# When q and k are transposed, and where four modulation vectors are made, in a two-layer transformer on one core

## The chip, the cores and the metric

The kernel runs on one core of one Trainium2 chip. The metric is the device time of one execution in microseconds (us), and the number to predict is its median over several runs.

## The reference, cut to what matters

Two layers work on 256 latent and 256 context tokens of width 1024. Six modulation vectors per layer come from a small matrix product with a 1024 x 6144 weight. Layer 0 is attention beside a convolution and a dense feed-forward stage; layer 1 is a state-space mixer (S5) and a mixture of experts.

```python
def adaln(cond, w, b):
    return jnp.split(jax.nn.silu(cond) @ w + b, 6, axis=-1)
...
def na_conv_mixer(h_lat, h_ctx, w_in, q_g, k_g, ...):
    def project(h):
        q, k, v, a, g = jnp.split(h @ w_in, [512, 1024, 1536, 2048], axis=-1)
        return rmsnorm(heads(q), q_g), rmsnorm(heads(k), k_g), heads(v), a, g
    ...
    y_lat = concat(neighbourhood_attention(ql, kl, vl, kc, vc, rpb), conv_module(al, gl, ...)) @ w_out
    y_ctx = concat(context_attention(qc, kc, vc), conv_module(ac, gc, ...)) @ w_out
...
for l in range(2):
    sh1, sc1, g1, sh2, sc2, g2 = adaln(c, ada_w[l], ada_b[l])
    ...
    x_lat = x_lat + g1 * y_lat
    x_lat = x_lat + g2 * ffn(modulate(rmsnorm(x_lat, norm2_g[l]), sh2, sc2))
```

## The kernel before

All matrix products of the big weights are done as three products of split operands (`mm3`, lines 223 to 225): a weight tile of 1 MB is cast on ScalarE (`wh`, line 203), and the rest of it (`wl`, line 205) is formed on VectorE or GpSimd. In the profile and here PE, DVE, ACT, POOL and SP are TensorE, VectorE, ScalarE, GpSimd and SyncE.

**Weights.** `Stream` hands out four buffers of 1 MB (`raw`). `plan` lists the loads in order; SP issues each as soon as a buffer is free, in that order. A buffer comes free when its weight has been split, or, for a modulation weight (`ada`), when PE has used it.

**Modulation vectors.** A vector (l, v) has two halves n, and a half two loads j of 1 MB: a *unit* (l, v, n, j). `ada_unit` does four matmuls of 32 x 512 on one unit, side by side in four column groups, into one PSUM bank `ada`; after j = 1 `ada_out` copies the bank to `adsb` on ACT (line 373), and `ada_to_dram` (line 435) writes the half to a scratch tensor by a DMA that ACT issues. The jobs wait in one list (`fill`), and `ada_step` takes the next if its load has been issued. The vectors (1, 2) to (1, 5) are needed after the feed-forward stage.

**The first projection** (`mix_in`): for n in 3, 4, 0, 1, 2 (a, g, q, k, v) and two halves kh of the depth, four steps k of 12 matmuls of 512 columns, into four banks `mi`; PSUM has eight banks. After g, `glu` transposes `aT` (`uT`, line 592) and the taps of the convolution begin (`conv`): 93 on DVE (lines 674 and 676, `cv`), 31 by ACT and POOL (`ptap`, line 685). After q and after k, ACT squares the four banks (line 655), DVE sums them (`qss`, line 656), forms a reciprocal root from small operations and multiplies the banks by it (`qn`, line 658); the banks stay taken until then. `turn_qk` then transposes `qn` on PE (`qT`, line 601) and ACT copies it (line 602). It is called in the middle of the next projection:

```python
if rest and k == 1 and (kh if n else not kh):
    rest()
```

**Order.** ACT, POOL and SP follow the program's text here (`ORDERED`, "mix"); PE and DVE are ordered by a scheduler when the kernel is built. Every engine then runs its queue strictly in that order. In attention (`scores`, `raised`, ...), twelve jobs each need maxima on DVE (line 760 or 765), and the rest of the taps and the units of layer 0 lie between.

**The feed-forward stage** (`ffn`): eleven steps u, each with w1 and w3, and w2 four times. Between them lie the tables of S5: `pool_job` on POOL (`bst`, line 1179), `dve_job` on DVE, `pe_job` on PE (`g1T`, line 1210, and `kk`, line 1219). Units are done after w1 of steps below `ADAU` and in the stage's tail (`tail`, `TAIL`).

Of the kernel before, what the change touches and what calls it, by code (L numbers as in the profile page):

```python
# [33 lines left out]
def unit(w, k0, nk):  # L34

    return w[:, k0:k0 + nk]
# [120 lines left out]
class Kernel:  # L157
# [80 lines left out]
    def plan(self):  # L238
        a, st = self.a, self.st
        self.g1d = self.dram.tile([P, 64 * 256], F32, name="g1d")  # L240
        self.g2d = self.dram.tile([P, 64 * 256], F32, name="g2d")
        self.rowsd = self.dram.tile([4, D], F32, name="rowsd")
        self.partd = self.dram.tile([4, 4 * D], F32, name="partd")
        self.gated = [[self.dram.tile(shape, F32, name="gated") for shape in ([4, 2 * D], [2, D])] for _ in range(2)]
        self.kd = self.dram.tile([16, 64 * 240], F32, name="kd")
        mi = lambda n, kh: st.add(("mi", n, kh), unit(a["mix_w_in"][n], 4 * kh, 4))
        mix = lambda n: [mi(n, kh) for kh in range(2)]
        part = lambda l, v, n, j: st.add(("ada", l, v, n, j), unit(a["ada_w"][l, 2 * v + n], 4 * j, 4))
        ada = lambda l, v: [part(l, v, n, j) for n in range(2) for j in range(2)]
        for n in range(2):  # L250
            for v in range(2):
                for j in range(2):
                    part(0, v, n, j)
            mi(3, n)
        mix(4), mix(0), mix(1), mix(2)
        for qt in range(2):
            st.add(("bias", qt), a["bias"][:, qt])
        ada(0, 2), ada(0, 3), ada(0, 4)
        for kh in (1, 0):
            for n in range(2):  # L260
                st.add(("mo", n, kh), unit(a["mix_w_out"][n], 4 * kh, 4))
        halves = [(l, v, n) for l, v in ((0, 5), (1, 0), (1, 1), (1, 2), (1, 3), (1, 4), (1, 5)) for n in range(2)]

        def half():
            l, v, n = halves.pop(0)
            for j in range(2):
                part(l, v, n, j)
        for u in range(11):
            st.add(("w1", u), a["ffn_w1"][u])
            if u < 9:  # L270
                half()
            st.add(("w3", u), a["ffn_w3"][u])
            if u < 3:
                half()
            if u in FFN_ENDS:
                lo, hi = FFN_ENDS[u]
                for n in range(2):
                    for f in range(lo, hi, 4):
                        st.add(("w2", f, n), unit(a["ffn_w2"][n], f, min(4, hi - f)))
        half(), half()  # L280
        for j in range(2):
            for kh in range(2):
                st.add(("si", j, kh), a["ssm_w_in"][j, kh].rearrange("p r k f -> p r (k f)"))
        for b in range(8):
            st.add(("g1", b), self.g1d[:, b * UNIT:(b + 1) * UNIT])
        k = self.kd
        add_k = lambda b: st.add(("k", b), bass.AP(tensor=k.tensor, offset=k.offset + b * 16 * 240,
                                                   ap=[[16, 8], [64 * 240, 16], [240, 16], [1, 128]]))
        add_g2 = lambda b: st.add(("g2", b), self.g2d[:, b * UNIT:(b + 1) * UNIT])
        def add_so(j, dh, *zs):  # L290
            for z in zs:
                st.add(("so", dh, j, z), a["ssm_w_out"][dh, j, z])
        add_so(0, 0, 0, 1)
        for b in range(2):
            add_k(b)
        for b in range(4):
            add_g2(b)
        for b in (2, 3):
            add_k(b)
        add_g2(4), add_g2(5)  # L300
        add_so(0, 1, 0)
        add_g2(6), add_g2(7)
        add_so(0, 1, 1)
        for dh in range(2):
            add_so(1, dh, 0, 1)
        self.moe_plan()
# [270 lines left out]
    def mix_in(self, second):  # L577
# [19 lines left out]
        def turn_qk(n, qn):  # L597
            for pr in range(4):
                pt = self.ps("qT")
                for t in range(4):  # L600
                    nc.tensor.transpose(pt[:, t * P:(t + 1) * P], qn[:, t, pr * P:(pr + 1) * P], self.ident)
                nc.scalar.activation(self.qk[:, n, pr], pt, AF.Copy, scale=gains[n])

        rest, first = None, []
        for i, (n, kh) in enumerate(order):
            for j in (i, i + 1) if i else ():
                if j < len(order):
                    self.split(("mi",) + order[j])
            if kh == 0:
                pb = [self.ps("mi") for _ in range(4)]  # L610
            for k in range(4):
                bh, bl = self.piece(("mi", n, kh), k, 0, 512)
                kk = kh * 4 + k
                for t in range(4):
                    s = slice(t * P, (t + 1) * P)
                    self.mm3(pb[t], self.hh[:, kk, s], self.hl[:, kk, s], bh, bl, kk == 0, kk == 7)
                    if not i:
                        for _ in range(START.count((k, t))):
                            second.pop(0)()
                        if (k, t) == SPLIT1:  # L620
                            self.split(("mi", 3, 1))
                if first:
                    first.pop(0)()
                if rest and k == 1 and (kh if n else not kh):
                    rest()
                    rest = None
                if i:
                    self.pump(t=10, v=MIXV[n] if n < 3 else 0, p=MIXP[n] if n < 3 else 0)
            if not i:
                self.load_params(nc.scalar)  # L630
            if not i:
                self.qk = mp.tile([P, 2, 4, 512], F32, name="qk", tag="qk")
                self.v = mp.tile([P, 4, 512], F32, name="v", tag="v")
            self.drop(("mi", n, kh))
            if kh == 0:
                continue
            if n == 3:
                for t in range(4):
                    nc.scalar.copy(aT[:, t], pb[t])
            elif n == 4:  # L640
                for t in range(4):
                    g = self.wk([P, 512], "gt", 2)
                    nc.scalar.activation(g, pb[t], AF.Tanh, scale=0.5)
                    nc.vector.scalar_tensor_tensor(aT[:, t], g, 1.0, aT[:, t], op0=OP.add, op1=OP.mult)
                rest = glu
            elif n == 2:
                for t in range(4):
                    nc.scalar.copy(self.v[:, t], pb[t])
            else:
                qn = mp.tile([P, 4, 512], F32, name="qn", tag="big")  # L650
                ss = self.wk([P, 32], "qss", 1)
                heads = lambda y: y.rearrange("p (h d) -> p h d", h=8)
                for t in range(4):
                    sq = self.wk([P, 512], "gt", 2)
                    nc.scalar.activation(sq, pb[t], AF.Square)
                    nc.vector.tensor_reduce(ss[:, t * 8:t * 8 + 8], heads(sq), axis=AX.X, op=OP.add)
                rs = self.rsqrt(ss, 32, 64)
                first = [lambda t=t, y=pb[t], q=qn, r=rs[:, t * 8:t * 8 + 8]: nc.vector.tensor_tensor(
                    heads(q[:, t]), heads(y), r[:, :, None].to_broadcast([P, 8, 64]), op=OP.mult) for t in range(4)]
                rest = lambda n=n, qn=qn: turn_qk(n, qn)  # L660
# [66 lines left out]
    def attention(self):  # L727
# [76 lines left out]
        n = len(jobs)  # L804
        soft, pTs, out = {}, {}, None
        fill = [(m, t) for m in range(2) for t in range(4)]
        for i in range(n + 3):
# [2 lines left out]
            if i - 2 in soft:  # L810
                pTs[i - 2] = turn_p(soft.pop(i - 2))
            ss = scores(*jobs[i]) if i < n else None
            if i and len(self.vec) < 6:
                self.ada_step()
            self.pump(v=TAPS[0], p=TAPS[1])
            if ss:
# [108 lines left out]
    def ffn(self, g2b, norm):  # L925
# [20 lines left out]
        for u in range(11):  # L946
            lo = max([0] + [hi for e, (_, hi) in FFN_ENDS.items() if e < u])
            for which in ("w1", "w3"):
# [8 lines left out]
                else:  # L957
# [5 lines left out]
                    banks.clear()  # L963
                if which == "w1" and u < ADAU or u < 3:
                    self.ada_step()
# [1219 lines left out]
    def layer0(self):  # L2185
# [3 lines left out]
        sh2 = self.const.tile([P, 2, 8, 2], F32, name="shsc2")  # L2189
        shs = self.const.tile([P, 2, 8, 2], F32, name="shsc3")  # L2190
        gates = lambda: self.gates
        self.ada_to_rows(0, 2, gates)
        for i, v in enumerate((3, 4)):
            self.ada_to_cols(0, v, sh2[:, i], C_AB + 16 + 8 * i)
        self.ada_to_rows(0, 5, gates)
        for i in range(2):
            self.ada_to_cols(1, i, shs[:, i], C_AB + 32 + 8 * i)
        for i, v in enumerate((2, 3, 4, 5)):
            self.ada_to_dram(1, v, i)
        with tc.tile_pool(name="l0", bufs=1) as self.l0:  # L2200
            self.s5_params(self.l0.tile([P, 32, 64], F32, name="room", tag="gates"))
            self.hh, self.hl = self.halves()
# [79 lines left out]
MIXP = (1, 1, 3)  # L2282
ADDS = ((0,), (1,), (2,), (3,), (4,), (5,))
TAIL = (0, 0, 2, 0, 1, 1)
ADAU = 10
EARLY = (4, ('si', 0, 0))
START = ((1, 3), (1, 3), (1, 3), (3, 1))
SPLIT1 = (2, 3)
# [34 lines left out]
```

## Time and profile before

| | us |
|---|---|
| median of 3 runs | 1869.29 (1868.2 to 1874.53) |
| the profiled execution's own time | 1870.19 |
| its span in the profile | 1868.4 |

The profile is of one execution. Engine times are busy times; a wait is put down to the instruction that ended it. The projection lies between about 45 and 185 us of the span, attention between 185 and 260, the feed-forward stage between 330 and 785, S5 and the experts behind it.

### The profile page before, as it was taken

To read this page: it belongs to the slowest core of one execution; us is meant where nothing else is said; L and a number is where in the kernel's file an instruction comes from. 1 tells how busy PE (TensorE), PEld (TensorE's weight loads), DVE (VectorE), ACT (ScalarE), POOL (GpSimd) and SP (SyncE) were. 2 spreads that over 40 slices of the span, in tenths; PEclk is the share of its full clock that TensorE was granted. 3 is DMA by queue.
4 is the path that set the end of the run, shared out by engine and by line. 5 is a ranking of instruction groups with operands and counts; after the bars stand their busy time and mean duration, and the time that the engine had idled before them with its cause. 6 is when DMAs were issued, how large, how long until landed. Compare 5 with 4: busy or idle time off the path is not lost.

```text
span 1868.4 us, 23796 instructions
## 1 busy us (share of the span) xinstructions
PE 1725.3 (92%) x8730; PEld 1188.6 (64%) x8730; DVE 1249.1 (67%) x1709; ACT 803.0 (43%) x1156; POOL 474.6 (25%) x528
## 2 busy tenths in 40 slices
PE   6977898998989999897589999999999999999997
PEld 4855376876767778675478666556565656565653
DVE  4999797576675754769788565656565656565653
ACT  3434664332332332547456445344543435443540
POOL 2347057395893900245241000000000000000000
PEclk9988999999999999998799999999999999999999
DMA  7320734753645543449868899999999999998996
GB/s 319 131 73 23 278 123 152 255 193 125 220 157 177 194 160 113 160 159 176 251 272 330 340 419 419 404 386 387 420 420 381 385 390 420 417 387 356 407 420 273
DMA packets 107437, 517.08 MB, mean 277 GB/s; under 512 B 13792, under 2 KB 41696, under 8 KB 48688
## 3 DMA queue, kind: packets, MB, share of 16 engines
q1 hardware_dynamic: 76672, 490.77, 68.5%
q10 hardware_dynamic: 29968, 22.57, 3.8%
q0 software_dynamic: 672, 2.14, 0.4%
q8 instruction: 71, 1.16, 0.2%
q14 instruction: 54, 0.44, 0.1%
HBM read 496.46 MB, written 18.97 MB: 276 GB/s over the span
## 4 chain that ended last, share of the span: by engine, by line
PE 56%; DVE 7%; POOL 2%; DMA 2%; issue 1%; ACT 1%; ACTq 0%; SPq 0%; DVEq 0%; POOLq 0%
PE m L2022 11%; PE m L223 5%; PE y L2056 5%; PE m L224 5%; PE m L225 5%; PE y L224 3%; PE y L223 3%; PE y L225 3%; PE w L224 3%; PE w L223 3%; PE w L225 3%; DVE wl L205 1%; PE xT L1850 1%; PE gT L2041 1%; PE sc L1940 1%
## 5 line engine op out<-in xcount | busy, mean ns | idle before, releaser
L203 ACT CAST wh<-raw 128x1024 fp32r<-128x1024 f32 x192 | 194.6, 1049 | 155.1 <-PE w L225 74.7
L205 DVE TENSOR_TENSOR wl<-raw,wh 128x1024 fp32r<-128x1024 f32 x171 | 215.9, 1298 | 37.2 <-ACT wh L203 37.0
L2022 PE MATMUL m<-raw,E 128*64 128x512 f32 x392 | 177.9, 596 | 0.0
L2044 ACT CAST small<-gT 128x512 fp32r<-128x512 f32 x28 | 16.4, 586 | 300.3 <-PE gT L2041 300.3
L224 PE MATMUL w<-hl,wh 128*128 128x512 f32 (+1 forms) x384 | 144.1, 375 | 1.2 <-POOL hl L568 0.6
L223 PE MATMUL w<-hh,wh 128*128 128x512 f32 (+1 forms) x384 | 145.2, 379 | 0.0
L225 PE MATMUL w<-hh,wl 128*128 128x512 f32 (+1 forms) x384 | 142.8, 373 | 0.0
L224 PE MATMUL m<-wl,small 128*128 128x512 f32 x336 | 131.1, 390 | 1.0 <-DVE wl L205 1.0
L223 PE MATMUL m<-wh,small 128*128 128x512 f32 x336 | 131.4, 391 | 0.0
L225 PE MATMUL m<-wh,small 128*128 128x512 f32 x336 | 130.8, 389 | 0.0
L2045 DVE TENSOR_TENSOR small<-gT,small 128x512 fp32r<-128x512 f32 x28 | 19.4, 692 | 156.8 <-ACT small L2044 156.8
L2022 PE MATMUL m<-xres,E 128*64 128x512 f32 x216 | 98.5, 598 | 0.0
L2022 PEld LDWEIGHTS m<-raw,E 128*64 128x64 f32 x392 | 51.0, 137 | 66.5 <-issue 66.4
L1844 POOL TENSOR_SCALAR brow<-pw,order 128x128 fp32r<-128x128 f32 x6 | 5.5, 930 | 310.2 <-PE bk L1879 310.2
L223 PEld LDWEIGHTS w<-hh,wh 128*128 128x128 f32 x384 | 72.7, 189 | 17.3 <-issue 4.0
L224 PEld LDWEIGHTS w<-hl,wh 128*128 128x128 f32 x384 | 72.8, 189 | 15.0 <-POOL hl L568 2.8
L224 PE MATMUL w<-wl,gh 128*128 128x512 f32 x176 | 72.1, 410 | 10.4 <-DVE wl L205 10.4
L225 PEld LDWEIGHTS w<-hh,wl 128*128 128x128 f32 x384 | 72.5, 189 | 12.9
L205 POOL TENSOR_TENSOR wl<-raw,wh 128x1024 fp32r<-128x1024 f32 x21 | 53.2, 2543 | 100.3 <-ACT wh L203 100.3
L205 DVE TENSOR_TENSOR wl<-U,wh 128x1024 fp32r<-128x1024 f32 x55 | 67.3, 1262 | 13.2 <-ACT wh L203 13.1
L223 PE MATMUL w<-wh,gh 128*128 128x512 f32 x176 | 71.8, 408 | 2.0 <-ACT wh L203 2.0
L223 PEld LDWEIGHTS m<-wh,small 128*128 128x128 f32 x336 | 63.1, 188 | 15.2 <-ACT more L203 2.3
(440 smaller groups left out, 4474.1 us busy)
## 6 DMA issues: line engine op xcount, KB each, us to landing
raw<-in_moe SPq DMA_DIRECT2D x134, 1024.0 KB, 10.1
U<-in_moe SPq DMA_DIRECT2D x70, 1024.0 KB, 9.8
room<-in_moe SPq DMA_DIRECT2D x68, 1024.0 KB, 8.4
raw<-in_ada_w SPq DMA_DIRECT2D x48, 1024.0 KB, 5.2
h<-in_moe SPq DMA_DIRECT2D x35, 1024.0 KB, 10.5
raw<-in_ffn_w SPq DMA_DIRECT2D x30, 1024.0 KB, 5.0
xres<-in_moe SPq DMA_DIRECT2D x29, 1024.0 KB, 9.9
raw<-in_mix_w_in SPq DMA_DIRECT2D x10, 1024.0 KB, 6.3
```

The costliest lines, as they stand in the source:

```text
L203: nc.scalar.copy(wh[:, :m], flat[:, h:h + m])
L205: eng.tensor_tensor(wl[:, :m], flat[:, h:h + m], wh[:, :m].bitcast(F32), op=OP.subtract)
L223: nc.tensor.matmul(o, lhsT=ah, rhs=bh, start=start, stop=False)
L224: nc.tensor.matmul(o, lhsT=ah, rhs=bl, start=False, stop=False)
L225: nc.tensor.matmul(o, lhsT=al, rhs=bh, start=False, stop=stop)
L1850: self.nc.tensor.matmul(pt[:, i * P:(i + 1) * P], lhsT=self.h2[:, t, (4 * n + i) * P:(4 * n + i + 1) * P], rhs=self.perm[:, e % 2, t].bitc ...
L1940: nc.tensor.matmul(po, lhsT=back[r, t].bitcast(F32), rhs=box[0][r], start=True, stop=True)
L2022: nc.tensor.matmul(o[64 * i:64 * i + 64], lhsT=self.few[:, 4 * j + k], rhs=w[i][:, k], start=not j and not k, stop=j == 1 and k == 3, tile ...
L2041: nc.tensor.transpose(pt[:, i * P:(i + 1) * P], g[:, i * P:(i + 1) * P], self.ident)
L2044: nc.scalar.copy(gh, v)
L2045: nc.vector.tensor_tensor(gl, v, gh.bitcast(F32), op=OP.subtract)
L2056: nc.tensor.matmul(y[64 * n:64 * n + 64], lhsT=t[:, 2 * j + f], rhs=w[:, f, n * 512:n * 512 + 512], start=not c and not j and not f, stop= ...
```

## The change

The call of `turn_qk` moves: for q and k it is made after the last step of the next projection (kh = 1, k = 3), not after that half's second step; for g it stays where it was. The 16 units of (1, 2) to (1, 5) leave the feed-forward stage (two after w1 of each of the steps 3 to 8, four in the tail). Their loads stand in the projection's list, four ahead of the second half of each of q, k, v, and four behind v; their jobs stand first in `fill`, and one is taken after each step k of the second half of the projections 4, 0, 1 and 2.

```diff
--- before.py
+++ after.py
@@ -252,14 +252,19 @@
                 for j in range(2):
                     part(0, v, n, j)
             mi(3, n)
-        mix(4), mix(0), mix(1), mix(2)
+        mi(4, 0)
+        for i, n in enumerate((4, 0, 1, 2)):
+            mi(n, 1)
+            if n != 2:
+                mi((n + 1) % 5, 0)
+            ada(1, 2 + i)
         for qt in range(2):
             st.add(("bias", qt), a["bias"][:, qt])
         ada(0, 2), ada(0, 3), ada(0, 4)
         for kh in (1, 0):
             for n in range(2):
                 st.add(("mo", n, kh), unit(a["mix_w_out"][n], 4 * kh, 4))
-        halves = [(l, v, n) for l, v in ((0, 5), (1, 0), (1, 1), (1, 2), (1, 3), (1, 4), (1, 5)) for n in range(2)]
+        halves = [(l, v, n) for l, v in ((0, 5), (1, 0), (1, 1)) for n in range(2)]
 
         def half():
             l, v, n = halves.pop(0)
@@ -267,7 +272,7 @@
                 part(l, v, n, j)
         for u in range(11):
             st.add(("w1", u), a["ffn_w1"][u])
-            if u < 9:
+            if u < 3:
                 half()
             st.add(("w3", u), a["ffn_w3"][u])
             if u < 3:
@@ -277,7 +282,6 @@
                 for n in range(2):
                     for f in range(lo, hi, 4):
                         st.add(("w2", f, n), unit(a["ffn_w2"][n], f, min(4, hi - f)))
-        half(), half()
         for j in range(2):
             for kh in range(2):
                 st.add(("si", j, kh), a["ssm_w_in"][j, kh].rearrange("p r k f -> p r (k f)"))
@@ -621,9 +625,11 @@
                             self.split(("mi", 3, 1))
                 if first:
                     first.pop(0)()
-                if rest and k == 1 and (kh if n else not kh):
+                if rest and ((kh, k) == (1, 3) if n else (kh, k) == (0, 1)):
                     rest()
                     rest = None
+                if i > 1 and kh:
+                    self.ada_step(1)
                 if i:
                     self.pump(t=10, v=MIXV[n] if n < 3 else 0, p=MIXP[n] if n < 3 else 0)
             if not i:
@@ -810,7 +816,7 @@
             if i - 2 in soft:
                 pTs[i - 2] = turn_p(soft.pop(i - 2))
             ss = scores(*jobs[i]) if i < n else None
-            if i and len(self.vec) < 6:
+            if i and len(self.vec) < 14:
                 self.ada_step()
             self.pump(v=TAPS[0], p=TAPS[1])
             if ss:
@@ -2189,14 +2195,14 @@
         sh2 = self.const.tile([P, 2, 8, 2], F32, name="shsc2")
         shs = self.const.tile([P, 2, 8, 2], F32, name="shsc3")
         gates = lambda: self.gates
+        for i, v in enumerate((2, 3, 4, 5)):
+            self.ada_to_dram(1, v, i)
         self.ada_to_rows(0, 2, gates)
         for i, v in enumerate((3, 4)):
             self.ada_to_cols(0, v, sh2[:, i], C_AB + 16 + 8 * i)
         self.ada_to_rows(0, 5, gates)
         for i in range(2):
             self.ada_to_cols(1, i, shs[:, i], C_AB + 32 + 8 * i)
-        for i, v in enumerate((2, 3, 4, 5)):
-            self.ada_to_dram(1, v, i)
         with tc.tile_pool(name="l0", bufs=1) as self.l0:
             self.s5_params(self.l0.tile([P, 32, 64], F32, name="room", tag="gates"))
             self.hh, self.hl = self.halves()
@@ -2282,7 +2288,7 @@
 MIXP = (1, 1, 3)
 ADDS = ((0,), (1,), (2,), (3,), (4,), (5,))
 TAIL = (0, 0, 2, 0, 1, 1)
-ADAU = 10
+ADAU = 3
 EARLY = (4, ('si', 0, 0))
 START = ((1, 3), (1, 3), (1, 3), (3, 1))
 SPLIT1 = (2, 3)
```

Three places, as the queues stand. Line numbers behind the change are 4 to 6 higher from `plan` and `mix_in` on: 338 is 334, 377 is 373, 439 is 435, 597 is 593, 649 is 643, 662 is 656.

**SP and ACT around projection 4.** SP's list of loads from the first one on, before:

```order
L85 DMA raw<-in_ada_w 128x2048 x4
L85 DMA raw<-in_mix_w_in 128x2048
L85 DMA raw<-in_ada_w 128x2048 x4
L85 DMA raw<-in_mix_w_in 128x2048 x9
L85 DMA raw<-in_bias 128x2048 x2
```

and now, with ACT's queue below it (`gt` at line 649 is the tanh of projection 4, `upad` the copy of `uT`):

```order
L85 DMA raw<-in_mix_w_in 128x2048 x4
L85 DMA raw<-in_ada_w 128x2048 x4
L85 DMA raw<-in_mix_w_in 128x2048 x2
L85 DMA raw<-in_ada_w 128x2048 x4
L85 DMA raw<-in_mix_w_in 128x2048 x2
L85 DMA raw<-in_ada_w 128x2048 x4
L85 DMA raw<-in_mix_w_in 128x2048
L85 DMA raw<-in_ada_w 128x2048 x4
L85 DMA raw<-in_bias 128x2048 x2
```

```order
L377 COPY adsb<-ada 128x512
L439 DMA partd<-adsb 4x512
L377 COPY adsb<-ada 128x512
L439 DMA partd<-adsb 4x512
L649 ACTIVATE gt<-mi 128x512 x4
L203 CAST wh<-raw 128x1024 x2
L597 ACTIVATE upad<-uT 128x2x256 x4
```

The first four units' loads take the places of the fifth to eighth projection loads, and two copies of modulation halves stand ahead of the tanh.

**DVE from the first taps to the sum of q's squares**, before:

```order
L205 TENSOR_TENSOR wl<-raw,wh 128x1024
L676 SCALAR_TENSOR_TENSOR cv<-upad,cols,cv 128x512 x11
L656 TENSOR_REDUCE qss<-gt 128x8 x2
L676 SCALAR_TENSOR_TENSOR cv<-upad,cols,cv 128x512
L656 TENSOR_REDUCE qss<-gt 128x8 x2
```

and now:

```order
L205 TENSOR_TENSOR wl<-raw,wh 128x1024
L682 SCALAR_TENSOR_TENSOR cv<-upad,cols,cv 128x512 x23
L662 TENSOR_REDUCE qss<-gt 128x8 x2
L682 SCALAR_TENSOR_TENSOR cv<-upad,cols,cv 128x512
L662 TENSOR_REDUCE qss<-gt 128x8 x2
```

Twelve more taps stand ahead of the sum. Ahead of the sum of k's squares it is 16 where it was 12, and ahead of the first maximum of attention 14 where it was 13: 86 of the 93 taps then lie before attention, where it was 69.

**PE near the end of projection 1 (k)**, now, with what each waits for:

```order
L225 MATMUL mi<-wh,hl 128x512
L338 MATMUL ada<-raw,sil 32x512 [waits DMAHW7_49,DVE_49]
L338 MATMUL ada<-raw,sil 32x512 x3
L338 MATMUL ada<-raw,sil 32x512 [waits DMAHW1_49]
L338 MATMUL ada<-raw,sil 32x512 x3
L223 MATMUL mi<-wh,hh 128x512
L224 MATMUL mi<-wl,hh 128x512
L225 MATMUL mi<-wh,hl 128x512
L338 MATMUL ada<-raw,sil 32x512 [waits DMAHW2_49,DVE_49]
```

The row ahead of the first unit is the 81st of the projection's 96 matmuls; 15 matmuls and a third unit follow, then the 16 transposes of q and a fourth unit. Before, the transposes stood behind the 72nd. In projection 2 the first unit stands behind the 79th matmul, and so do the rest. In projections 4 and 0 a unit stands behind the 60th, 72nd, 84th and 96th matmul.

## Rows read from the trace of the kernel before

**Rows 1.** The page: span and busy time of each engine.
```profile
span 1868.4 us, 23796 instructions
PE 1725.3 (92%) x8730; PEld 1188.6 (64%) x8730; DVE 1249.1 (67%) x1709; ACT 803.0 (43%) x1156; POOL 474.6 (25%) x528
```

**Rows 2.** Busy time by stretch: stretch, length, engines (x instructions), clock, DMA share, GB/s.
```profile
60.00:80.00 20.00, 20.00 (x89) 16.54 (x89) 19.62 (x92) 4.79 (x6) 7.17 (x3) 1.00 0.23 83
88.00:187.00 99.00, 72.73 (x315) 57.96 (x317) 96.58 (x120) 42.48 (x62) 58.19 (x32) 0.84 0.16 53
184.00:260.00 76.00, 66.50 (x498) 36.43 (x497) 62.78 (x138) 54.45 (x128) 6.88 (x6) 0.98 0.68 237
```

**Rows 3.** Timeline of PE: start, us, instructions, [idle before, what ended it].
```profile
86.35 1.91 PE L592 MATMUL uT<-ident,aT 128*128 128x128 f32 x16
...
134.78 4.83 PE L601 MATMUL qT<-ident,qn 128*128 128x128 f32 x16 [12.86 <-DVE qn L658]
...
173.44 4.83 PE L601 MATMUL qT<-ident,qn 128*128 128x128 f32 x16 [11.98 <-DVE qn L658]
...
184.78 1.14 PE L742 MATMUL S<-qk 64*128 64x256 f32 x8
...
186.71 1.92 PE L334 MATMUL ada<-raw,sil 128*32 128x512 f32 x16
```

**Rows 4.** Busy time of PE in a stretch behind q's wait: length, busy, clock.
```profile
136.00:138.00 2.00, 1.88 (x8) 0.50 0.94 365
```

**Rows 5.** Timeline of DVE, from the first tap to attention's first maximum.
```profile
87.85 2.77 DVE L674 TENSOR_SCALAR cv<-upad,cols 128x512 f32<-128x512 f32 x2 [0.22 <-ACT upad L593]
...
104.81 7.38 DVE L676 SCALAR_TENSOR_TENSOR cv<-upad,cols,cv 128x512 f32<-128x512 f32 x11
112.10 1.28 DVE L656 TENSOR_REDUCE qss<-gt 128x8 f32<-128x512 f32 x2
...
134.05 2.47 DVE L658 TENSOR_TENSOR qn<-mi,ny 128x512 f32<-128x512 f32 x4
...
146.89 1.28 DVE L656 TENSOR_REDUCE qss<-gt 128x8 f32<-128x512 f32 x2 [2.42 <-ACT gt L655]
...
172.71 2.47 DVE L658 TENSOR_TENSOR qn<-mi,ny 128x512 f32<-128x512 f32 x4
...
186.81 1.27 DVE L760 TENSOR_REDUCE nm<-S 128x2 f32<-128x512 f32 x2
```

**Rows 6.** Timeline of SP's DMA issues, 70 to 100 us.
```profile
82.02 8.23 SPq L85 DMA_DIRECT2D raw<-in_mix_w_in  x2
```

**Rows 7.** The page, DMA issues: count, size, us to landing.
```profile
raw<-in_ada_w SPq DMA_DIRECT2D x48, 1024.0 KB, 5.2
```

**Rows 8.** Timeline of ACT: squares of q, and a copy of a modulation half.
```profile
102.61 1.28 ACT L655 ACTIVATE gt<-mi 128x512 f32<-128x512 f32 x2 [3.23 <-PE mi L225]
...
190.93 0.58 ACT L373 COPY adsb<-ada 128x512 f32<-128x512 f32 x1
```

**Rows 9.** Timeline of PE in the feed-forward stage: units, and a wait for POOL.
```profile
463.22 1.92 PE L334 MATMUL ada<-raw,sil 128*32 128x512 f32 x16
...
540.01 0.98 PE L1210 MATMUL g1T<-ident,g1t 128*128 128x128 f32 x7 [0.81 <-POOL g1t L1153]
...
596.22 1.92 PE L334 MATMUL ada<-raw,sil 128*32 128x512 f32 x16
...
768.55 1.92 PE L334 MATMUL ada<-raw,sil 128*32 128x512 f32 x16
777.48 1.06 PE L334 MATMUL ada<-raw,sil 128*32 128x512 f32 x8
```

**Rows 10.** Timeline of POOL, table jobs of the feed-forward stage's second burst.
```profile
467.43 0.62 POOL L1179 COPY bst<-bb 64x128 f32<-64x128 f32 x2 [22.16 <-PE kk L1219]
...
509.53 1.50 POOL L1179 COPY bst<-bb 64x128 f32<-64x128 f32 x2
...
526.98 1.50 POOL L1179 COPY bst<-bb 64x128 f32<-64x128 f32 x2
```

## The prediction

> **What bounds the kernel now.** The page comes first: PE is busy for 92% of the span [rows 1], but that is a mean over stages. The table of stretches says more. In the projection (88 to 187 us) PE is busy for 72.7 of 99 us, DVE for 96.6: DVE is the bound there, PE waits for it. In attention (184 to 260) PE is busy for 66.5 of 76 us, DVE for 62.8: neither has much to spare, PE less [rows 2]. PE's timeline shows where it stood in the projection: 12.86 and 11.98 us ahead of the two groups of `qT` transposes, both ended by DVE's `qn` [rows 3]. DVE's timeline shows why: its queue is full of taps, and the chain from `qss` to `qn` lies in it [rows 5].
>
> So two things are to be asked of the change: does work put into PE's waits come free, and does DVE get later?
>
> **Unit prices.** 89 matmuls in 20.00 us make 0.225 us for one [rows 2]. Two units took 1.92 us [rows 3], so one is 0.96. A tap is 7.38/11 = 0.67 [rows 5]. A load of 1 MB lands in 5.2 us [rows 7]. A copy of a modulation half takes 0.58 on ACT, a square of q 0.64 [rows 8]. The 16 loads move past SP's other loads without filling the DMA engines: their share was 0.16 in the projection [rows 2]. POOL's queue is unchanged. Eight ACT copies (4.6 us) move into a stretch in which ACT was busy for 42.5 of 99 us [rows 2]; their length costs nothing, their place does, as follows.
>
> **Projection 4: +7.2.** The fourth unit's load needs the buffer whose place was free at 82.02, when SP issued the next load [rows 6]. It lands at 82.0 + 5.2 = 87.2; PE does the unit until 88.2, then 24 matmuls (5.4) and `uT` at 93.6, where it was 86.35 [rows 3]. The tanh of projection 4 waits too, since the copy of that half stands ahead of it on ACT, but 93.6 is the later. DVE has only the four products for `aT` and one weight to do meanwhile, so its first tap moves from 87.85 [rows 5] to 95.1. The loads of (0, 1) and (1, 0) are queued on SP behind that load; they are used over 10 us later and hide.
>
> **q: +8.0 more.** DVE has 12 more taps ahead of q's sum: 12 x 0.67 = 8.0. The sum starts at 112.10 + 7.2 + 8.0 = 127.3. Its squares are not what it waits for: the last unit of projection 0 gets its buffer when DVE has split (1, 0), just ahead of the taps (104.81 + 7.2 = 112.0 [rows 5]), lands at 117.2, is done at 118.2, and its copy and the square end by 119.5. The chain to `qn` keeps its ten taps, so `qn` starts at 134.05 + 15.2 = 149.3.
>
> PE starts projection 1 at 118.2 and reaches the first unit behind 81 matmuls (18.2) at 136.4, or some 2 us later if the weight of the second half holds it up. That unit needs a PSUM bank; q's four are held until `qn`. One quarter of `qn` (0.6) ends at 149.9. So PE waits some 11 us, where it waited 12.86: the units meant for the wait stand behind it. Then come three units, 15 matmuls, 16 transposes and a unit: 2.9 + 3.4 + 1.9 + 1.0 = 9.2 at the full clock. After q's wait the clock was at 0.50, 1.2 GHz [rows 4], and 16 transposes took 4.83 where `uT` took 1.91 [rows 3]; I add that 2.9. PE ends at 162.0.
>
> The Trainium skill (Perfetto Trace Analysis, Optimization Strategy) says that a gap that keeps coming back on the engine that should be full can mean that no SBUF or PSUM is left for the next tile. The row names DVE's `qn`; here both hold, since `qn` frees the bank. With a spare bank the three units would fit into the wait, k's sum would wait only for DVE's taps, and attention would start some 1.6 us earlier: a sum of +7 in place of +9.
>
> **k: +2 more.** The squares of k stand on ACT behind the copy of the last unit (162.0 + 0.6), a tap's part (0.7) and take 0.6: 163.9. DVE has done `qn` and 16 taps at 149.3 + 2.5 + 10.7 = 162.5, so it idles for 1.4 (2.42 before). k's sum starts at 163.9 against 146.89 [rows 5]: +17.0. `qn` starts at 189.7, PE goes on at 190.3 after another wait of some 10 us, and with two matmuls more ends the same tail at 202.8: the first `S` of attention, 184.78 before [rows 3]. DVE's first maximum moves by 17.0 and one tap to 204.5, from 186.81 [rows 5]. Both say **+18**. The bias loads are queued behind the last four units, at some 192 us, and land before attention adds them.
>
> **Attention: -3.** 17 of 24 taps are gone from it, 11.4 us of DVE. PE's work there is the same: twelve jobs, twelve units. PE's idle time, 76 - 66.5 = 9.5 us [rows 2], is the most it can give back; nothing is the least, and a loss of 2 if the units' loads, now late, hold it up. I take 3, nearer to nothing, because PE was at 88% and its waits are short ones.
>
> **Feed-forward stage: -6.** Seven pairs of 1.92 and two single units of 1.06 [rows 9], 15.6 us of PE, leave. Three pairs count in full: the one at 463 stands ahead of the `kk` that lets POOL begin its burst of table jobs (467.43 [rows 10]); the one at 596 stands the same way ahead of the third burst; the one at 768 is in the tail with nothing beside it. Inside a burst POOL takes 526.98 - 509.53 = 17.5 us for a job [rows 10], and PE, with the pairs at 491 and 520 in it, still had to wait 0.81 at 540.01 [rows 9]. Without them PE waits longer there; I count these two pairs, and the two like them in the third burst, at nothing, though at most 7.7 if POOL has slack. The single units filled waits for DVE: nothing, at most 2.1. So 3 x 1.92 = 5.8, at most 15.6. Loads of 16 MB less in this stage cost and give nothing: no wait for a load ends a PE wait there that I found.
>
> **Sum.** +18 - 3 - 6 = +9. The profiled execution took 1870.19, so 1879; it lay 0.9 above the median of the runs shown, which makes **1878**.
>
> **Rivals.** 0.3% of this kernel, 5.6 us, is about what a measurement can tell from no change.
>
> *DVE's taps are only moved.* If attention hangs on DVE's queue, it gives back all 11.4 us of the 17 taps: 18 - 11.4 - 6 = +0.6, 1870, no change. For it: DVE was busy for 83% there, and some of its maxima stand behind taps. Against: PE cannot give back more than 9.5. It decides where attention shrinks by more than 6.
>
> *The waits take the units (faster).* The feed-forward stage gives back all 15.6, POOL's jobs getting shorter or having slack, and attention 9.5: 18 - 9.5 - 15.6 = -7, 1862. It decides from the place where PE reaches the second and third burst's transposes: if POOL is 4 us early there, the pairs count. For it: POOL was late by only 0.81 at one of them. Against: that is late, not early. The Trainium skill (Perfetto Trace Analysis, Optimization Strategies) holds that the matmul engine should be kept as busy as possible; by that rule the units belong into PE's 24.8 us of waits, and this case is its outcome.
>
> *Loads late in attention.* The bias and the first units of layer 0 have two buffers, and now start some 60 us later; if PE and DVE wait for them, attention does not shrink but grows by 5: 18 + 5 - 6 = +17, 1887. Against: two loads of 5.2 us against jobs of 6 us.
>
> **Numbers.** The forecast has 0.58, its own range 1871 to 1886 (half of its doubts are the size of attention's gain); 0.05 of it counts as no change. Only moved: 0.21, of which 0.17 no change, 0.02 faster, 0.02 slower. Units taken: 0.13, of it 0.12 faster, 0.01 no change. Loads late: 0.08, slower. Faster 0.14, no change 0.23, slower 0.63. The range leaves out most of the case "units taken" and the far end of the last: 1865 to 1888.
>
> **What would show it.** Right: `uT` at about 93 us; DVE idle for some 6 us ahead of it; 23 taps in one run; PE still idle for about 10 us twice, now ended at a modulation unit by `qn`; first `S` at 200 to 205; PE's waits for POOL or DVE at the tables grown to 3 or 4 us. Wrong: `S` before 195; waits below 5 us; a feed-forward stage shorter by over 10 us; attention shorter by over 6.

## The result, and the profile after

| | before | changed |
|---|---|---|
| median, us (10 runs each) | 1872.38 | 1881.38 |
| the profiled execution, us | 1870.19 | 1878.22 |
| its span, us | 1868.4 | 1876.4 |

The changed kernel is slower: the ratio is 1.0053, with a 95% interval of 1.0040 to 1.0067, some 9.9 us (the medians differ by 9.0). The forecast was +9. The rows below answer to those read before.

The page (answers to [rows 1]):

```profile
span 1876.4 us, 23786 instructions
PE 1721.6 (92%) x8730; PEld 1180.4 (63%) x8730; DVE 1253.0 (67%) x1709; ACT 801.4 (43%) x1156; POOL 483.1 (26%) x528
```

The shares say nothing: the same work, 8 us longer. PE's timeline says where (start, us, instructions, idle before; answers to [rows 3]):

```profile
85.97 1.94 PE L338 MATMUL ada<-raw,sil 128*32 128x512 f32 x8 [2.62 <-DMA raw<-in_ada_w]
...
94.03 1.91 PE L596 MATMUL uT<-ident,aT 128*128 128x128 f32 x16
...
147.96 3.22 PE L338 MATMUL ada<-raw,sil 128*32 128x512 f32 x16 [10.87 <-DVE qn L664]
...
155.85 2.03 PE L605 MATMUL qT<-ident,qn 128*128 128x128 f32 x16
...
189.29 3.64 PE L338 MATMUL ada<-raw,sil 128*32 128x512 f32 x16 [12.27 <-DVE qn L664]
...
199.03 2.03 PE L605 MATMUL qT<-ident,qn 128*128 128x128 f32 x16
...
201.99 1.13 PE L748 MATMUL S<-qk 64*128 64x256 f32 x8
...
242.01 1.93 PE L338 MATMUL ada<-raw,sil 128*32 128x512 f32 x8 [4.48 <-DMA raw<-in_ada_w]
```

PE waited 24.84 us for `qn` in two places before and waits 23.14 now, at a unit in place of the transposes: the units stand behind the waits, not in them. The fourth unit of projection 4 waits for its load, and `uT` comes at 94.03 in place of 86.35.

DVE's timeline, from the products for `aT` to attention's first maximum (answers to [rows 5]):

```profile
89.78 2.65 DVE L650 SCALAR_TENSOR_TENSOR aT<-gt,aT 128x512 f32<-128x512 f32 x4 [7.65 <-ACT gt L649]
...
95.30 1.58 DVE L680 TENSOR_SCALAR cv<-upad,cols 128x512 f32<-128x512 f32 x2 [1.40 <-ACT upad L597]
...
107.93 17.39 DVE L682 SCALAR_TENSOR_TENSOR cv<-upad,cols,cv 128x512 f32<-128x512 f32 x23
125.23 1.27 DVE L662 TENSOR_REDUCE qss<-gt 128x8 f32<-128x512 f32 x2
...
147.23 2.47 DVE L664 TENSOR_TENSOR qn<-mi,ny 128x512 f32<-128x512 f32 x4
149.62 10.68 DVE L682 SCALAR_TENSOR_TENSOR cv<-upad,cols,cv 128x512 f32<-128x512 f32 x16
162.72 1.28 DVE L662 TENSOR_REDUCE qss<-gt 128x8 f32<-128x512 f32 x2 [2.42 <-ACT gt L661]
...
188.55 2.47 DVE L664 TENSOR_TENSOR qn<-mi,ny 128x512 f32<-128x512 f32 x4
190.95 12.52 DVE L682 SCALAR_TENSOR_TENSOR cv<-upad,cols,cv 128x512 f32<-128x512 f32 x14
203.38 1.28 DVE L766 TENSOR_REDUCE nm<-S 128x2 f32<-128x512 f32 x2
```

DVE idles 7.65 us for the tanh of projection 4, which on ACT stands behind the copy of that late unit. Then 23 taps run in one piece ahead of q's sum. Attention starts 17.2 us later than before (201.99 against 184.78).

Attention itself, from first `S` to last `O`, by stretch (length, engines, clock, DMA share, GB/s), the kernel before:

```profile
184.80:259.60 74.80, 65.30 (x493) 35.68 (x493) 61.66 (x137) 53.40 (x125) 6.88 (x6) 0.98 0.69 241
```

and the changed one:

```profile
202.00:280.20 78.20, 66.38 (x497) 36.20 (x493) 50.51 (x119) 54.88 (x130) 6.88 (x6) 0.93 0.73 245
```

DVE has 11 us less to do (50.51 against 61.66), yet attention takes 3.4 us more in this pair of profiles, at a granted clock of 0.93 where it was 0.98. So the end of attention is 20.6 us late. The rest gives back: from last `O` to the first product of S5 (`si`) the kernel before took 522.5 us and the changed one 512.2; from there to PE's last matmul 1077.4 and 1074.9. Sum: 17.2 + 3.4 - 10.3 - 2.5 = 7.8, for 8.0 of span.

### The profile page after: what moved, and what is told of

The parts are those of the page before. It is cut to its first block, busy times and chain, and to the rows that moved or that the text cites. A ratio compares the mean times of both kernels' runs of the same rounds, so it can differ in the third digit from the quotient of the medians.

```text
span 1876.4 us, 23786 instructions
## 1 busy us (share of the span) xinstructions
PE 1721.6 (92%) x8730; PEld 1180.4 (63%) x8730; DVE 1253.0 (67%) x1709; ACT 801.4 (43%) x1156; POOL 483.1 (26%) x528
## 4 chain that ended last, share of the span: by engine, by line
PE 53%; DVE 8%; DMA 2%; POOL 2%; issue 1%; ACT 1%; SPq 0%; DVEq 0%; POOLq 0%; ACTq 0%
PE m L2028 11%; PE m L223 5%; PE y L2062 5%; PE m L225 5%; PE m L224 5%; PE y L223 3%; PE y L224 3%; PE y L225 3%; PE w L223 2%; PE w L225 2%; PE w L224 2%; DVE wl L205 1%; PE xT L1856 1%; PE gT L2047 1%; PE sc L1946 1%
## 5 line engine op out<-in xcount | busy, mean ns | idle before, releaser
L205 DVE TENSOR_TENSOR wl<-raw,wh 128x1024 fp32r<-128x1024 f32 x171 | 221.5, 1331 | 37.6 <-ACT wh L203 36.0
L338 PE MATMUL ada<-raw,sil 128*32 128x512 f32 x384 | 54.5, 664 | 30.5 <-DVE qn L664 23.1
## 6 DMA issues: line engine op xcount, KB each, us to landing
raw<-in_mix_w_in SPq DMA_DIRECT2D x10, 1024.0 KB, 10.3
```

Source lines behind the costliest of these rows:

```text
L205: eng.tensor_tensor(wl[:, :m], flat[:, h:h + m], wh[:, :m].bitcast(F32), op=OP.subtract)
L338: self.nc.tensor.matmul(pa[32 * j:32 * j + 32], lhsT=self.sil[:, k], rhs=rhs, start=k < 4, stop=k >= 4, tile_position=(0, 32 * j))
```

## The experiments

All twelve, by the same four marks, read from PE's timeline of each kernel's profiled execution; the ratio is to the kernel before, with its interval.

| kernel | uT | first S | S to last O | last O to si | ratio |
|---|---|---|---|---|---|
| before | 86.35 | 184.78 | 74.84 | 522.53 | |
| changed | 94.03 | 201.99 | 78.19 | 512.20 | 1.0053 (1.0040 to 1.0067) |
| e1 late transposes alone | 85.16 | 179.51 | 83.67 | 521.03 | 1.0007 (0.9998 to 1.0016) |
| e2 units alone | 95.76 | 204.46 | 75.40 | 508.91 | 1.0061 (1.0046 to 1.0076) |
| e3 late transposes, no units | 86.69 | 181.03 | 85.56 | 511.89 | 0.9972 (0.9957 to 0.9987) |
| e4 no units | 84.78 | 182.76 | 78.41 | 513.06 | 0.9966 (0.9953 to 0.9978) |
| e5 changed, two more loads | 94.59 | 201.62 | 77.06 | 511.98 | 1.0043 (1.0023 to 1.0062) |
| e6 before, two more loads | 84.97 | 182.93 | 75.56 | 521.15 | 0.9971 (0.9962 to 0.9981) |
| e7 two units in projection 4 | 87.20 | 195.15 | 81.72 | 511.11 | 1.0033 (1.0021 to 1.0045) |
| e8 late transposes, two more loads | 85.79 | 180.15 | 81.19 | 518.25 | 0.9996 (0.9985 to 1.0007) |
| e9 loads without the units | 86.69 | 185.19 | 78.87 | 518.21 | 0.9993 (0.9981 to 1.0005) |
| e10 four units at the boundary | 84.95 | 186.03 | 77.08 | 513.11 | 0.9972 (0.9962 to 0.9983) |
| e11 and pairs in FFN waits | 85.10 | 184.99 | 77.49 | 512.50 | 0.9991 (0.9979 to 1.0004) |
| e12 e10 with late transposes | 85.04 | 181.74 | 81.37 | 514.29 | 0.9985 (0.9972 to 0.9997) |

One profile is one execution: `uT` lies between 84.78 and 86.69 in the kernels that change nothing ahead of it, and the way from `si` to PE's last matmul between 1074.9 and 1079.4 in all fourteen. A difference of 2 us between two rows of one column is thus no finding. Attention is less steady still. In the kernel before, e4 and e9 the queues of PE, DVE and ACT are the same, instruction for instruction, up to its end, and it takes 74.84, 78.41 and 78.87 us; in e2 and the changed kernel, which differ only ahead of it, 75.40 and 78.19. By stretch, e2 and e9:

```profile
204.46:279.86 75.40, 64.62 (x496) 35.49 (x493) 50.27 (x118) 54.73 (x129) 6.88 (x6) 0.98 0.76 256
185.19:264.06 78.87, 67.70 (x493) 36.93 (x493) 61.68 (x137) 53.30 (x126) 6.89 (x6) 0.94 0.66 228
```

The time goes with the granted clock, 0.98 in the short ones and 0.93 to 0.94 in the long ones, and not with the change: the three kernels with all 16 units in the projection (changed, e2, e5) have a mean of 76.9, and so have the four with DVE's 11 us still in attention and the transposes where they were (before, e4, e6, e9).

### The two halves of the change apart: e1 and e2

e1, against the kernel before:

```diff
-                if rest and k == 1 and (kh if n else not kh):
+                if rest and ((kh, k) == (1, 3) if n else (kh, k) == (0, 1)):
```

> The kernel before with the late transposes alone; the units stay in the feed-forward stage. Theory A (the loss comes from the units in the projection, the late transposes are no part of it): DVE's chain for q stays where it was, k's sum starts within 0.5 us of 146.9, and only 9 taps stand between k's qn and attention's first maximum where 13 stood, 4 x 0.67 = 2.7 us; behind k's qn PE has 16 transposes to do and no longer 24 matmuls of v. First S at 180 to 181 (184.78 before), the kernel 3 to 5 us faster than before. Theory B (the late transposes are what makes attention late): first S later than 188, the kernel slower than before by 3 us or more.

e2 is the same edit undone in the changed kernel.

> The changed kernel with the transposes called where they were before; the units stay in the projection. Theory A: the transposes still stand behind the first unit that waits for qn, so nothing is won: first S at 201 to 204, the kernel within 3 us of the changed one, 0.4 to 0.7% over before. Theory B: first S at 195 or earlier, the kernel no slower than before.

First `S` came 5.3 us earlier in e1, as theory A has it, but the kernel is no faster. Attention took all of it. PE's timeline of e1 at attention's start:

```profile
174.60 4.82 PE L601 MATMUL qT<-ident,qn 128*128 128x128 f32 x16 [11.29 <-DVE qn L658]
179.51 1.49 PE L742 MATMUL S<-qk 64*128 64x256 f32 x7
...
188.79 1.49 PE L783 MATMUL PT<-ident,prob 128*128 128x128 f32 x6 [4.57 <-ACT prob L775]
```

its DVE:

```profile
176.26 9.07 DVE L676 SCALAR_TENSOR_TENSOR cv<-upad,cols,cv 128x512 f32<-128x512 f32 x9
185.26 1.27 DVE L760 TENSOR_REDUCE nm<-S 128x2 f32<-128x512 f32 x2
```

and its first 20 us of attention by stretch, in two halves, with the kernel before's below:

```profile
179.50:189.50 10.00, 5.42 (x32) 2.23 (x32) 10.00 (x17) 6.84 (x19) 1.90 (x2) 1.00 0.50 182
189.50:199.50 10.00, 10.00 (x33) 3.71 (x31) 8.02 (x18) 6.96 (x16) 0.00 (x0) 0.50 0.24 69
184.80:204.80 20.00, 16.40 (x114) 7.25 (x114) 17.50 (x36) 13.19 (x36) 0.00 (x0) 0.91 0.59 201
```

`S` is early, but nine taps, 1.0 us each here, stand ahead of DVE's first maximum, at 185.26 against 186.81 [rows 5]: of the 5.3 us 1.5 are left. In between PE has little to do, 5.42 of the first 10 us, and waits 4.57 for `prob`. Behind that wait the clock granted is 0.50 (1.2 GHz, where 1.00 is 2.4 GHz) for 10 us. Over the first 20 us that makes 0.75, where the kernel before has 0.91; e3, e8 and e12, which also have the late transposes, have 0.75, 0.68 and 0.73. Besides, the 24 matmuls of v between transposes and `S` had stood in part where the clock was low (0.80 in the 7 us ahead of `S`). What the taps cost and what the clock costs was not taken apart.

e2 is as slow as the changed kernel, and its first `S` as late. Theory A holds: the whole loss belongs to the units, and beside them the place of the transposes is worth nothing, since they wait behind a unit that waits for `qn`.

### What the units cost in the feed-forward stage: e3, e4, e9

e3 and e4 leave the 16 units out of the changed kernel (e4 with the transposes where they were), with loads and jobs; the rows they would have filled are written from other halves:

```diff
-            ada(1, 2 + i)
...
-                if i > 1 and kh:
-                    self.ada_step(1)
...
-        for i, v in enumerate((2, 3, 4, 5)):
-            self.ada_to_dram(1, v, i)
```

> The late transposes, and the 16 units of (1, 2) to (1, 5) left out everywhere, with their loads: that part is not computed. Against e1 this is the price of the units in the feed-forward stage. The prediction's term (three pairs count): 6 us faster than e1. What the trace of the changed kernel reads like (12.6 us between the end of attention and the end of the feed-forward stage less 1.6 of a clock difference): 10 to 12 us faster than e1. First S as in e1.

> The kernel before with the same 16 units left out: that part is not computed. First S as before (184 to 185). Prediction's term: 6 us faster than before; reading of the changed trace: 10 to 12 us faster. If e4 differs from before as e3 from e1, the price of the units in the feed-forward stage does not hang on when the stage begins.

By the ratios the price is 0.34 to 0.35%, some 6.5 us; but without these vectors the experts' stage works on other numbers, so the stage itself is the better measure. From last `O` to `si`, e1, e6, e8 and the kernel before, with units there, take 518.3 to 522.5, mean 520.7; the changed kernel, e2, e3, e4, e5 and e7, without, 508.9 to 513.1, mean 511.5. The price is **9.2 us**, between the term of the prediction (6) and the first reading of the trace (10 to 12), nearer to the reading.

e9 keeps the loads in the stage, but one matmul per unit and no copies:

```diff
+            if l and v > 1:
+                self.idle(l, v, n, j)
+                return
```

> The kernel before with all 16 loads of (1, 2) to (1, 5) kept in the feed-forward stage, but only one matmul of each unit's four, and without the copies and the writes of the halves: the vectors are not computed. From last O to the first product of S5 the kernels with these units in the stage took 522.5, 521.0, 521.2 and 518.3 us, those without 508.9 to 513.1. Theory P (the units cost PE's time there): 511 to 515. Theory D (their 16 MB cost, since the tables' writes to DRAM land later beside them): 517 to 522.

This one missed what it was made for. PE's timeline of e9, a pair of units:

```profile
468.53 1.90 PE L374 MATMUL ada<-raw,sil 128*32 128x512 f32 x4
```

Two matmuls (the profile counts each twice) take 1.90 us where eight took 1.92 [rows 9], so no time of PE was taken away, and at 518.2 the kernel is with those with units, at their lower edge, its ratio at 0.9993. It tells the loads from PE's time in nothing. It does show one thing. In the kernel before, POOL starts the second burst of table jobs at 467.43 [rows 10] and then waits 6.51 us for a write to DRAM (6.63 in the third burst):

```profile
474.56 0.34 POOL L1180 COPY g2t<-braw 128x64 f32<-128x64 f32 x1 [6.51 <-DMA g2d<-g2t]
```

That write is issued by ACT, behind the copy of a half and its own write. ACT before:

```profile
465.21 0.59 ACT L373 COPY adsb<-ada 128x512 f32<-128x512 f32 x1 [1.29 <-PE ada L334]
465.82 0.54 ACTq L435 DMA_DIRECT2D partd<-adsb  x1
466.41 0.45 ACTq L1203 DMA_DIRECT2D g2d<-g2t  x1
```

POOL in the changed kernel, at the same place:

```profile
483.78 0.62 POOL L1185 COPY bst<-bb 64x128 f32<-64x128 f32 x2 [20.13 <-PE kk L1225]
485.09 0.23 POOL L1186 COPY g2t<-braw 128x64 f32<-128x64 f32 x1 [0.69 <-DVE kt L1232]
```

and in e9:

```profile
472.72 0.62 POOL L1194 COPY bst<-bb 64x128 f32<-64x128 f32 x2 [20.65 <-PE kk L1234]
473.39 0.24 POOL L1195 COPY g2t<-braw 128x64 f32<-128x64 f32 x1
```

Where the copy and its write are gone, with or without the loads, so is the wait at this place; one of 1.8 to 4.9 us is left a job later. From ACT's issue to POOL's read the write took 8.15 us before (466.41 to 474.56); in the changed kernel, where ACT issues it at 481.69, POOL reads 3.40 us later. So most of the wait is the write itself being slow, and not its place in ACT's queue; no run shows why.

What the wait is worth can be read from POOL's rows, where the second burst opens (above) and where the third does, in the kernel before and in e9:

```profile
600.43 0.62 POOL L1179 COPY bst<-bb 64x128 f32<-64x128 f32 x2 [22.44 <-PE kk L1219]
...
602.22 0.62 POOL L1194 COPY bst<-bb 64x128 f32<-64x128 f32 x2 [21.56 <-PE kk L1234]
```

From opening to opening that is 133.0 and 129.5 us. The four kernels with units in the stage take 132.4 to 133.0, the six without 126.8 to 129.4: e9, with PE's pairs and the loads but no copies, is next to the latter. So some 3 us go with the copies and writes in this burst. e9 does not show it in its total, since its second burst opens 208.7 us behind last `O`, later than in all others (203.4 to 207.8); no run shows why.

### Attention: e5, e6, e8

Two more loads of layer 0 find room at attention's start, in the tile `hl`, which stands empty until the third job:

```diff
+                spare = self.l0.tile([P, 2, UNIT], F32, name="spare", tag="hl")
+                self.st.lend(spare[:, 0], spare[:, 1], once=True)
...
+            if i == 3:
+                self.yl = self.l0.tile([P, 8, 512], F32R, name="hl", tag="hl")
```

> The changed kernel with room for two more loads at the start of attention: the third and fourth unit of layer 0 land in the place of the tile hl, which stands empty until attention's third job, so the two loads do not wait for one of the two buffers that the bias leaves. Nothing ahead of attention moves. Theory L (attention is late by 3.4 us because its units wait for loads): first S at 202 as in the changed kernel, no wait of over 1 us for a unit's load in attention, where there was one of 4.48; last O 3 to 5 us earlier, at 275 to 277; the kernel 3 to 5 us faster than the changed one. Rival C (what makes attention long is PE at the lower clock and the chain of maxima, the load wait only fills time that would be lost anyway): last O within 1 us of 280, and the time the same.

> The kernel before with the same room for two more loads. Theory L: the waits of 0.35, 0.25, 1.72 and 0.27 us for loads in attention go, 2 to 3 us in all, and last O is at 256.5 to 258 (259.62 before); the kernel is 0 to 3 us faster. Rival C: last O within 1 us of 259.6.

> The late transposes alone (units in the feed-forward stage), with room for two more loads at the start of attention. With the late transposes alone first S came 5.3 us earlier and last O 3.6 us later. Theory L (the gain was lost to loads that cannot start earlier): first S at 179 to 181, the wait of 3.43 us goes, last O at 258 to 260, the kernel 2 to 4 us faster than before. Rival K (the gain was lost to the clock, since PE now goes from its wait of 11 us straight into attention, at 0.75 of the clock for the first 20 us): last O at 262 to 264, no gain.

In e5 the wait is nearly as long as in the changed kernel, 3.55 against 4.48:

```profile
240.87 1.53 PE L338 MATMUL ada<-raw,sil 128*32 128x512 f32 x8 [3.55 <-DMA raw<-in_ada_w]
```

Last `O` moves by 1.5 us and the ratio stays within the interval: theory L in its form (too few buffers) falls. The loads do start late. SP's issues, before:

```profile
187.83 36.35 SPq L85 DMA_DIRECT2D raw<-in_ada_w  x10
```

and changed:

```profile
191.28 2.04 SPq L85 DMA_DIRECT2D raw<-in_bias  x2
196.31 48.03 SPq L85 DMA_DIRECT2D raw<-in_ada_w  x12
```

Before, the bias and two units had landed in the quiet projection. Now these four are queued behind units that wait for `qn`. But the late start does not explain the wait. The unit that PE waits for at 242.01 is the tenth of attention's twelve. Its load was issued at 231.77, and beside it ACT issued the second of two transfers of 512 KB (`gates`); before, the same unit waits 1.72, to 222.73, and its load stands beside the same transfer:

```profile
231.77 0.33 SPq L85 DMA_DIRECT2D raw<-in_ada_w  x1
231.79 0.35 ACTq L431 DMA_DIRECT2D gates<-gated  x1
...
215.44 0.33 SPq L85 DMA_DIRECT2D raw<-in_ada_w  x1
215.46 0.35 ACTq L427 DMA_DIRECT2D gates<-gated  x1
```

From issue to the end of the wait that is 10.2 us now and 7.3 before, where a load took 5.2 [rows 7]. And e9, whose loads start as in the kernel before, waits nearly as long for that unit as the changed kernel:

```profile
223.51 1.94 PE L334 MATMUL ada<-raw,sil 128*32 128x512 f32 x8 [4.19 <-DMA raw<-in_ada_w]
```

So a wait of 4 us for this load is part of the spread of attention, with or without the change. No run moved the `gates` transfers.

e6 beats the kernel before: 0.9971. Its rows don't show by what, since attention took 75.56 us in its profile. In e8 the two loads don't save the gain of the late transposes, which is the result that rival K has; first `S` at 180.15 and attention of 81.19 are like e1's.

### The late fourth load: e7

Two units behind projection 4, and the other two go to attention:

```diff
-            ada(1, 2 + i)
+            for _ in range((2, 4, 4, 6)[i]):
+                part(*early.pop(0))
...
-                if i > 1 and kh:
+                if i > 1 and kh and (n, k > 1) != (4, True):
```

> The changed kernel with only two units behind projection 4 instead of four (the other two go to attention); the late fourth load is taken away, and the orders of PE and DVE behind uT are the same as in the changed kernel. Theory A (a third of the delay is the load that PE and ACT wait for): uT at 88.3 to 89 (94.03 in the changed kernel, 86.35 before), q's sum and first S earlier by the same 5 to 6 us, S at 196 to 197; attention has two more units and gives back some of it: the kernel 2 to 5 us faster than the changed one. Rival (DVE makes up for the wait later, since it only has taps to do): first S within 2 us of 202, the time the same.

PE's timeline of e7:

```profile
87.20 1.91 PE L598 MATMUL uT<-ident,aT 128*128 128x128 f32 x16
...
195.15 1.13 PE L750 MATMUL S<-qk 64*128 64x256 f32 x8
```

Both are 6.8 us earlier than in the changed kernel, with the same order of taps behind: the delay of `uT` goes through to first `S` undiminished, and theory A holds. Attention with 14 units takes 3.5 us more in this profile and gives half of it back; the ratio is 1.0033 in place of 1.0053.

### Can a wait of PE take units? e10, e11, e12

e10 makes the four units of (1, 2) between projections 0 and 1, while four banks are still free, drops the pairs behind steps 3 and 6 of the feed-forward stage, and has the room for two loads:

```diff
-        mix(4), mix(0), mix(1), mix(2)
+        mix(4), mix(0), mi(1, 0), ada(1, 2), mi(1, 1), mix(2)
...
+            if (n, kh) == (1, 0):
+                self.ada_step(4)
...
-                if which == "w1" and u < ADAU or u < 3:
+                if which == "w1" and u < ADAU and u not in (3, 6) or u < 3:
```

> The kernel before with room for two more loads in attention, and with the four units of (1, 2) made between projections 0 and 1, where PE then waits for nothing but their loads and DVE's qn is 30 us away; the pairs behind steps 3 and 6 leave the feed-forward stage. The transposes stay in the middle of the next projection. If a unit is free only where no bank and no load holds it up and DVE's taps ahead of q's sum stay 11: q's sum and first S within 1.5 us of those with two more loads alone (S 182.9), the way from last O to S5 shorter by 2 to 4 us, the time 0.9945 to 0.996 of before. If PE's waits take no unit at all, first S later by 4 us or more and no gain over 0.997.

PE's timeline of e10:

```profile
108.38 1.06 PE L334 MATMUL ada<-raw,sil 128*32 128x512 f32 x8 [2.46 <-DMA raw<-in_ada_w]
...
133.01 4.63 PE L601 MATMUL qT<-ident,qn 128*128 128x128 f32 x16 [4.87 <-DVE qn L660]
```

The wait for q's `qn` shrinks from 12.86 to 4.87 and the transposes are no later: here the wait took the units, and a wait for their loads with them. The stage behind is 8 us shorter than in e6 (513.11 against 521.15), for two pairs. But DVE was given 15 taps ahead of k's sum where it had 12, and first `S` is 3.1 later than in e6 (attention, 1.5 longer, is within its spread). The ratio is e6's, 0.9972, and not the 0.9945 to 0.996 that was expected: the four units won nothing that the runs can tell.

e11 also puts two pairs ahead of the first `w2` products of steps 2 and 5; e12 is e10 with the late transposes.

> As the kernel with four units at the boundary, and two of the four pairs left in the steps of the feed-forward stage stand ahead of the first w2 products of steps 2 and 5, where PE waits 5 us for DVE's wl each time. If the waits take them: the two waits for wl shorter by some 2 us each, 2 to 4 us less from last O to S5, the time 0.993 to 0.9955 of before. If the loads of w2, now queued around the units, come later: no gain over the kernel before it in this list.

> The kernel with four units at the boundary, with the late transposes beside them. If the late transposes give back their gain to the clock and the loads: 0 to 3 us slower than with the transposes in the middle, 0.996 to 0.998 of before. If the four units at the boundary, with PE's 24 matmuls more before its wait for qn, use the place better: 2 us or more faster than with the transposes in the middle.

e11's stage is no shorter than e10's (512.5) and its ratio is back at 0.9991, against 0.993 to 0.9955 expected. Its one profile does not explain that: it is of the fastest of its runs, 1862.2 us with a median of 1868.1. e12 is between, 0.9985, some 2 us slower than e10, as expected of late transposes that gain nothing. So e6, the smallest edit, and e10 beat the kernel before by some 0.28%, and the changed one by more.

## Why the prediction was right, and where only in sum

- **Projection 4** held: `uT` at 94.03 for 93.6 forecast, and e7 shows that the last two of the four units, with the late load, are the cause.
- **q and k** held: sums at 125.2 and 162.7 (127.3 and 163.9 forecast), `qn` at 147.2 and 188.6 (149.3 and 189.7), waits of 10.87 and 12.27 at a unit, first `S` at 201.99 (202.8). The +18 is +17.2. The Trainium skill (Perfetto Trace Analysis, Optimization Strategy) says that a repeated gap can mean a lack of PSUM. e10 is in line with that, since four units placed where banks are free shorten the wait by 8.0 us.
- **Attention: -3** did not come. The step that failed is the one that took a part of PE's idle time as given back when taps leave DVE: DVE lost the 11 us and nothing came of it, 76.9 us by the mean with the change and 76.9 without. So attention does not hang on DVE's taps, and the rival "only moved" falls with it. The +3.4 of the two profiles is within the spread of kernels that change nothing there, 74.84 to 78.87, and goes with the clock. The rival "loads late", which had 0.08, has a wait of 4.48 for a load on its side, but e9 has one of 4.19 without late loads, and e2, whose loads start as late, takes 75.40: a cost of the late loads is not shown. What holds attention at its length stays open.
- **Feed-forward stage: -6** was too small: 10.3 between the two profiles, 9.2 over all kernels. More than 10 was among the signs of a wrong forecast, and it was this term that was off. The term that was mis-sized is the pair ahead of a burst, counted at PE's 1.92. e10 and e12, without those two pairs alone, take 513.7 on average, 7.0 less than 520.7: 3.5 for a pair. With a pair goes POOL's wait of 6.5 us at the burst's opening, which I had in no row; e9 puts it at some 3 us in the second burst. The other twelve units are worth about 2 together, so counting pairs inside a burst at nothing was near, and PE's wait for DVE in the second burst's `kk` did grow, from 1.63 to 4.14. The tail's pair, counted in full, brought little: from the last `kk` to `si` 121.95 before and 120.88 changed.
- **Sum**: +9 for 9.9 measured. That the sum came out is luck in part: over the kernels the term of attention was off by +3.0 (0 for -3) and that of the feed-forward stage by -3.2 (-9.2 for -6), and these cancel. PE's busy time from 88 to 187 us, 72.73 before [rows 2], rose:

```profile
88.00:187.00 99.00, 77.19 (x367) 55.53 (x367) 93.09 (x122) 42.13 (x62) 60.79 (x27) 0.91 0.46 168
```

The Trainium skill's advice to keep the matmul engine as busy as possible (Perfetto Trace Analysis, Optimization Strategies) was met by this, and the kernel lost. The same section says to optimize the engine that blocks the critical path when the matmul engine waits; here that was DVE, and the change put 12 more taps ahead of its sum of q.

## What to carry to other kernels

Work moved into an engine's wait is free only if it can start there: ask for the PSUM bank, the buffer and the load it needs at that moment, and for what its load displaces in the queue. A small step ahead of a chain on another engine can cost more than its own time (here 3.5 us for 1.92), when a write that the chain waits for comes behind the step's own copy and write. When a sum comes out right, look at its terms: here two wrong ones hid each other, and only stage marks over many kernels showed it. Those marks also showed which difference between two profiles was none: attention's 3.4 us.

## What the runs showed of the hardware that was not expected

One matmul of 32 columns takes as long as four of them side by side: 1.90 us for two units with one each, 1.92 with four each. And a short wait inside a stage can cost the clock behind it: in e1 a wait of 4.57 us was followed by 10 us at 0.50. PE being busy ahead of the stage does not rule that out. In e7 PE had no gap in the 7 us ahead of first `S`, at full clock, and yet the first 20 us of attention, with a wait of 1.76 in them, have 0.74:

```profile
188.15:195.15 7.00, 7.00 (x46) 4.29 (x45) 7.00 (x10) 2.33 (x4) 1.21 (x1) 1.00 0.87 320
195.15:215.15 20.00, 18.24 (x92) 7.87 (x88) 12.65 (x28) 13.60 (x34) 0.00 (x0) 0.74 0.61 216
```
